# One over the softmax sums by the vector engine's reciprocal, in the attention of a hybrid encoder trunk

## The chip, the cores and the metric

The kernel runs on one core of a Trainium2 chip. The metric is the device time of one execution in microseconds (us). The core's engines each work through a queue of their own in order: TensorE (PE in the rows, PEld for its weight loads), the vector engine (DVE), the scalar engine (ACT), GpSimd (POOL), and the sync engine (SP), which issues the transfers.

## The reference

The program is a trunk of two layers over 1024 tokens of width 1024, in float32. Layer 0 mixes tokens by grouped-query attention, layer 1 by a gated linear attention; a squared-ReLU MLP follows each. The change lies in the attention alone:

```python
def block(qblk):
    s = jnp.einsum('bqhgd,bkhd->bhgqk', qblk, k, preferred_element_type=jnp.float32) * scale
    p = jax.nn.softmax(s, axis=-1).astype(v.dtype)
    return jnp.einsum('bhgqk,bkhd->bqhgd', p, v)
```

There are 16 query heads of width 64 and 4 key/value heads. The softmax of a row of scores is exp(s - max) divided by its sum; the division is what the change is about.

## The kernel before, in words

**Tiling.** The attention handles one head and one half of the queries (512 of 1024) at a time: 16 heads by 2 halves are 32 units, here called halves. A half has eight steps, one for each chunk of 128 keys. In a step `scores` lets TensorE write the scores of 128 keys by 512 queries into a PSUM bank `ps_a` (two matmuls, L389 and L390). ACT takes the exponential twice, once rounded into `ph` (L396) and once in full into `p` (L397), and `pl = p - ph` is made by DVE for even chunks and by POOL for odd ones (L400). Three steps later `values` multiplies `ph` and `pl` with the values (three matmuls, L109 to L111) and adds the result up in a bank `ps_c`, of which there are two.

**The end of a half.** The value matrix has 64 columns of ones beside its 64 value columns. So after the eighth chunk the bank holds the outputs on 64 partitions (`orow`) and the sum of the exponentials on the other 64 (`srow`), each 512 wide. The end of `values` divides one by the other (L423 to L427), rounds the quotient into `dst_h` (L429, named `oh` in the rows), moves it to other partitions for half of the heads (L432) and keeps the remainder in `dst_l` (L434, `ol`).

**The maxima ahead.** The row maximum that the softmax subtracts is found by a sweep of its own, 22 steps ahead (`LEAD`): `max_step` is one matmul (L276) into a bank `ps_b` (two of them), for every third into `ps_a` (four, shared with the scores), and a DVE reduction of 128x512 (L277). There are sixteen for a head, one for each step, so eight for a half; they stop when the last head has its maxima. `max_end` (L281 to L286) turns a head's maxima round by a small transposition (L283).

**What sets the order.** The code issues steps in the order of the loops, and a scheduler at build time then sorts each engine's queue. The order on every engine is fixed before the run. Four tiles each of `ph` and `pl` and three of `p` are in use in turn.

Of the kernel before, what the change touches and what calls it, by code (L numbers as in the profile page):

```python
# [25 lines left out]
AF = mybir.ActivationFunctionType  # L26
ALU = mybir.AluOpType
# [22 lines left out]
def trunk_kernel(tc, xT, wqk, wv, wo, win0, wout0, gqk, gv, gvz, gr, gate, gwo, win1, wout1, cols, rope, cmat, yT):  # L50
    nc = tc.nc
# [4 lines left out]
    with ExitStack() as top:  # L56
# [35 lines left out]
        def bank(tag):  # L92
            return psum.tile([P, HN], F32, tag=tag, name="ps_" + tag, bufs=PS_BUFS[tag])
# [14 lines left out]
        def mm3(ps, wh, wl, xh, xl, start, stop):  # L108
            nc.tensor.matmul(ps, wh, xh, start=start, stop=False)  # L109
            nc.tensor.matmul(ps, wh, xl, start=False, stop=False)  # L110
            nc.tensor.matmul(ps, wl, xh, start=False, stop=stop)  # L111
# [80 lines left out]
        with ExitStack() as at:  # L192
# [210 lines left out]
            def values():  # L403
                h, half, c, phh, pll = queue.pop(0)
                g = h // 4
                if c == 0:
                    out_bank[0] = bank("c")
                po = out_bank[0]
                two = slice(g % 2, g % 2 + 2)
                mm3(po, va[:, c, g // 2, two].rearrange("p a d -> p (a d)"), vb[:, c, g // 2, two].rearrange("p a d -> p (a d)"),  # L410
                    phh, pll, c == 0, c == NCH - 1)
                if c < NCH - 1:
                    return
                if h % 2 == 0:
                    oh[h // 2][half] = big.tile([P, HN], F32R, tag="hi", name="oh")
                    ol[h // 2][half] = big.tile([P, HN], F32R, tag="lo", name="ol")
                dst_h, dst_l = oh[h // 2][half], ol[h // 2][half]
                r0 = env.tmp.tile([P, HN], F32, tag="rs_r", name="r0")
                tt = env.tmp.tile([P, HN], F32, tag="rs_t", name="tt")

                top_, bot = slice(0, 64), slice(64, P)
                orow, srow = (bot, top_) if g % 2 else (top_, bot)
                nc.scalar.activation(out=r0[srow], in_=po[srow], func=AF.Ln)  # L423
                nc.scalar.activation(out=r0[srow], in_=r0[srow], func=AF.Exp, scale=-1.0)
                nc.vector.tensor_tensor(out=tt[srow], in0=po[srow], in1=r0[srow], op=ALU.mult)
                nc.vector.scalar_tensor_tensor(out=tt[orow], in0=tt[srow], scalar=-2.0, in1=r0[srow], op0=ALU.add, op1=ALU.mult)
                nc.vector.scalar_tensor_tensor(out=r0[orow], in0=po[orow], scalar=-1.0, in1=tt[orow], op0=ALU.mult, op1=ALU.mult)  # L427
                rows = bot if h % 2 else top_
                nc.scalar.copy(out=dst_h[rows], in_=r0[orow])  # L429
                src = r0  # L430
                if rows != orow:
                    nc.scalar.copy(out=tt[rows], in_=r0[orow])  # L432
                    src = tt
                nc.vector.tensor_tensor(out=dst_l[rows], in0=src[rows], in1=dst_h[rows].bitcast(F32), op=ALU.subtract)  # L434
# [3 lines left out]
            for step in range(256):  # L438
                h = step // 16
                scores(h, step // 8 % 2, step % 8)  # L440
                while unit < min(256, step + LEAD):
                    n, i = unit // 16, unit % 16
                    if i == 0:
                        if n % 4 == 0:
                            load_k(n // 4)
                        load_q(n)
                    max_step(n, i)
                    if i == 15:
                        max_end(n)
                    unit += 1  # L450
                if len(queue) > LAG:
                    values()
                if step == 200:
                    ahead = [load_w(wo[m]) for m in range(3)]
            begun = [proj("b", ahead[m], (oh, ol), 0) for m in range(2)]
            while queue:
                values()
# [817 lines left out]
```

## Time and profile before

| | |
|---|---|
| median of 3 runs | 2357.78 us (2353.15 to 2358.01) |
| the profiled execution's own time | 2352.89 us |
| span of its profile | 2350.8 us |
| TensorE's mean granted clock | 0.994 of full speed |
| busy over the span | TensorE 98%, DVE 76%, ACT 57%, POOL 14% |
| first and last line L425 (one for each half) | 195.65 and 559.4 us |

The busy share is a mean over stages with different limits. TensorE's matmuls are pipelined and their ends are modelled, so a matmul that starts every 0.23 us shows a duration of 0.4 us: starts, not durations, tell its pace. The span is 2.1 us shorter than the execution's time, for what lies before the first and after the last instruction.

### The profile page before, as it was taken

How to read it: one execution, taken by the hardware profiler on the slowest of the kernel's cores; microseconds unless marked ns; L12 is line 12 of the kernel's file. 1: busy time of each engine (PE TensorE's matmuls, PEld its weight loads, DVE VectorE, ACT ScalarE, POOL GpSimd, SP SyncE). 2: the span in 40 equal slices, each digit the busy share in tenths (PEclk: the TensorE clock that was granted, in tenths of full speed). 3: DMA queues.
4: the chain of work that ended last, by engine and by line, in shares of the span. 5: the costliest groups of instructions: out<-in, count | busy, mean ns of one | idle time of the engine just before them, and what ended most of it. 6: DMA issues, size and time to landing. Idle time of an engine off the chain costs nothing. (4 is left out here: it accounts for less than half of the span.)

```text
span 2350.8 us, 29858 instructions
## 1 busy us (share of the span) xinstructions
PE 2292.8 (98%) x10710; PEld 1898.6 (81%) x10710; DVE 1777.5 (76%) x2502; ACT 1341.4 (57%) x2386; POOL 333.2 (14%) x267
## 2 busy tenths in 40 slices
PE   8889999999999999999999999999999999999996
PEld 6677777777878888888888888898878888888885
DVE  8999999995786556888776767667696655897785
ACT  7458999994465555433344865655455555543343
POOL 2444444443000000000012000000100000000003
PEclk9999999999999999999999999999999999999998
DMA  4442112104445456954422121125625545965422
GB/s 173 135 146 64 42 41 52 30 14 165 132 160 180 152 175 228 320 166 160 153 99 81 47 74 54 55 72 187 220 91 194 177 152 182 331 204 177 154 89 72
DMA packets 157796, 317.50 MB, mean 135 GB/s; under 512 B 15048, under 2 KB 17872, under 8 KB 157520
## 3 DMA queue, kind: packets, MB, share of 16 engines
q1 hardware_dynamic: 157648, 315.60, 40.2%
q8 instruction: 84, 1.38, 0.2%
q14 instruction: 64, 0.52, 0.1%
HBM read 223.20 MB, written 92.27 MB: 134 GB/s over the span
## 5 line engine op out<-in xcount | busy, mean ns | idle before, releaser
L97 DVE TENSOR_TENSOR wl<-raw,wh 128x1024 fp32r<-128x1024 f32 x293 | 361.0, 1232 | 198.4 <-ACT wh L96 197.0
L96 ACT CAST wh<-raw 128x1024 fp32r<-128x1024 f32 x293 | 307.4, 1049 | 327.7 <-PE ps_a L466 130.6
L96 ACT CAST hh<-hst 128x512 fp32r<-128x512 f32 x224 | 134.9, 618 | 246.1 <-PE ps_a L467 112.4
L147 POOL TENSOR_TENSOR sq<-sq 128x512 f32<-128x512 f32 x35 | 54.6, 1560 | 1373.7 <-ACT sq L145 772.6
L400 POOL TENSOR_TENSOR pl<-p,ph 128x512 fp32r<-128x512 f32 x128 | 178.9, 1397 | 190.4 <-ACT p L397 136.4
L465 PE MATMUL ps_a<-xh,wh 128*128 128x512 f32 x512 | 199.6, 391 | 2.5 <-ACT xh L96 2.5
L467 PE MATMUL ps_a<-xh,wl 128*128 128x512 f32 x512 | 199.8, 391 | 1.8 <-DVE wl L97 1.8
L97 DVE TENSOR_TENSOR hl<-hst,hh 128x512 fp32r<-128x512 f32 x224 | 153.1, 703 | 62.9 <-ACT hh L96 62.1
L466 PE MATMUL ps_a<-xl,wh 128*128 128x512 f32 x512 | 200.5, 392 | 0.0
L465 PE MATMUL ps_a<-hh,wh 128*128 128x512 f32 x512 | 199.3, 389 | 1.1 <-ACT h L505 1.1
L466 PE MATMUL ps_a<-hl,wh 128*128 128x512 f32 x512 | 199.3, 389 | 0.6 <-DVE hl L97 0.6
L467 PE MATMUL ps_a<-hh,wl 128*128 128x512 f32 x512 | 199.2, 389 | 0.0
L396 ACT ACTIVATE ph<-ps_a 128x512 fp32r<-128x512 f32 x248 | 149.0, 601 | 22.2 <-PE ps_a L390 19.7
L397 ACT ACTIVATE p<-ps_a 128x512 f32<-128x512 f32 x256 | 153.1, 600 | 1.0 <-POOL pl L400 0.2
L465 PE MATMUL ps_b<-xh,wh 128*128 128x512 f32 x384 | 149.5, 389 | 0.2 <-DVE s L560 0.2
L467 PE MATMUL ps_b<-xh,wl 128*128 128x512 f32 x384 | 149.4, 389 | 0.0
L466 PE MATMUL ps_b<-xl,wh 128*128 128x512 f32 x384 | 149.4, 389 | 0.0
L277 DVE TENSOR_REDUCE mx<-ps_b 128x1 f32<-128x512 f32 x181 | 121.9, 682 | 7.6 <-PE ps_b L276 5.5
L505 ACT ACTIVATE s<-s 128x512 f32<-128x512 f32 x96 | 60.6, 631 | 105.9 <-DVE s L560 105.9
L465 PEld LDWEIGHTS ps_a<-xh,wh 128*128 128x128 f32 x512 | 96.4, 189 | 23.2 <-ACT xh L96 3.3
L467 PEld LDWEIGHTS ps_a<-xh,wl 128*128 128x128 f32 x512 | 96.5, 188 | 23.1 <-DVE wl L97 2.7
L465 PEld LDWEIGHTS ps_a<-hh,wh 128*128 128x128 f32 x512 | 96.1, 188 | 21.8 <-ACT h L505 1.7
(280 smaller groups left out, 6038.0 us busy)
## 6 DMA issues: line engine op xcount, KB each, us to landing
raw<-in_win_dram SPq DMA_DIRECT2D x80, 512.0 KB, 3.8
raw<-in_wout_dram SPq DMA_DIRECT2D x80, 512.0 KB, 3.9
hst<-hid_dramFalse SPq DMA_DIRECT2D x56, 512.0 KB, 3.8
hst<-hid_dramTrue SPq DMA_DIRECT2D x56, 512.0 KB, 3.5
q<-q_dram SPq DMA_DIRECT2D x96, 128.0 KB, 2.9
hid_dramFalse<-s SPq DMA_DIRECT2D x48, 256.0 KB, 2.1
hid_dramFalse<-t SPq DMA_DIRECT2D x48, 256.0 KB, 3.1
hid_dramTrue<-s SPq DMA_DIRECT2D x48, 256.0 KB, 2.0
```

The lines of the kernel that those rows point to most:

```text
L96: nc.scalar.copy(out=hi, in_=src)
L97: (leng or nc.vector).tensor_tensor(out=lo, in0=src, in1=hi.bitcast(F32), op=ALU.subtract)
L147: self.eng.tensor_tensor(out=sq, in0=self.acc, in1=sq, op=ALU.add)
L277: nc.vector.tensor_reduce(out=mx[h][:, half * 8 + c : half * 8 + c + 1], in_=ps, axis=AX.X, op=ALU.max, negate=True)
L396: nc.scalar.activation(out=phh, in_=ps, func=AF.Exp)
L397: nc.scalar.activation(out=p, in_=ps, func=AF.Exp)
L400: (nc.vector if c % 2 == 0 else nc.gpsimd).tensor_tensor(out=pll, in0=p, in1=phh.bitcast(F32), op=ALU.subtract)
L465: nc.tensor.matmul(ps, wh, xh, start=start and i == 0, stop=False, skip_group_check=not start)
L466: nc.tensor.matmul(ps, wh, xl, start=False, stop=False, skip_group_check=not start)
L467: nc.tensor.matmul(ps, wl, xh, start=False, stop=i == len(parts) - 1, skip_group_check=not start)
L505: nc.scalar.activation(out=t, in_=src, func=AF.Relu)
```

## The change

The logarithm and the exponential on ACT (L423, L424) go, and so do the three DVE instructions of the two Newton steps (L425 to L427). In their place DVE takes the reciprocal of the sums straight from the PSUM bank, from partitions `srow` into `tt` on partitions `orow`, and then multiplies the bank's outputs with it.

```diff
                 orow, srow = (bot, top_) if g % 2 else (top_, bot)
-                nc.scalar.activation(out=r0[srow], in_=po[srow], func=AF.Ln)
-                nc.scalar.activation(out=r0[srow], in_=r0[srow], func=AF.Exp, scale=-1.0)
-                nc.vector.tensor_tensor(out=tt[srow], in0=po[srow], in1=r0[srow], op=ALU.mult)
-                nc.vector.scalar_tensor_tensor(out=tt[orow], in0=tt[srow], scalar=-2.0, in1=r0[srow], op0=ALU.add, op1=ALU.mult)
-                nc.vector.scalar_tensor_tensor(out=r0[orow], in0=po[orow], scalar=-1.0, in1=tt[orow], op0=ALU.mult, op1=ALU.mult)
+                nc.vector.reciprocal(tt[orow], po[srow])
+                nc.vector.tensor_tensor(out=r0[orow], in0=po[orow], in1=tt[orow], op=ALU.mult)
                 rows = bot if h % 2 else top_
                 nc.scalar.copy(out=dst_h[rows], in_=r0[orow])
```

The two new lines are L423 and L424 of the changed kernel; the lines behind them stand three lower than before (the cast L429 is L426 there, the remainder L434 is L431). The queues change only within the attention; what comes ahead of it and behind it is the same, instruction for instruction, on every engine. Inside it, here is the queue of DVE at the end of the third half before the change, from one `pl` to the remainder:

```order
L400 TENSOR_TENSOR pl<-p,ph 128x512
L277 TENSOR_REDUCE mx<-ps_b 128x1
L425 TENSOR_TENSOR tt<-ps_c,r_2161 64x512
L277 TENSOR_REDUCE mx<-ps_b 128x1
L426 SCALAR_TENSOR_TENSOR tt<-tt,r_2161 64x512
L400 TENSOR_TENSOR pl<-p,ph 128x512
L427 SCALAR_TENSOR_TENSOR r_2161<-ps_c,tt 64x512
L277 TENSOR_REDUCE mx<-ps_a 128x1
L277 TENSOR_REDUCE mx<-ps_b 128x1
L434 TENSOR_TENSOR ol<-tt,oh 64x512
```

And the queue of DVE at the same place in the changed kernel:

```order
L400 TENSOR_TENSOR pl<-p,ph 128x512
L277 TENSOR_REDUCE mx<-ps_b 128x1
L423 RECIPROCAL tt<-ps_c 64x512
L281 TENSOR_TENSOR mx<-mx 128x8
L400 TENSOR_TENSOR pl<-p,ph 128x512
L424 TENSOR_TENSOR r_2155<-ps_c,tt 64x512
L277 TENSOR_REDUCE mx<-ps_b 128x1 x2
L431 TENSOR_TENSOR ol<-tt,oh 64x512
```

The three instructions that were spread between reductions and a `pl` are now two, with the reciprocal directly ahead of `max_end` and of a `pl`; what stands behind it, reductions and `pl` alike, is as many as before.

The second place is ACT's queue at the end of the same half, before:

```order
L423 ACTIVATE r_2161<-ps_c 64x512
L396 ACTIVATE ph<-ps_a 128x512
L285 CAST row<-ps_b 8x128
L424 ACTIVATE r_2161<-r_2161 64x512
L397 ACTIVATE p<-ps_a 128x512
```

and in the changed kernel, up to the cast of the quotient:

```order
L396 ACTIVATE ph<-ps_a 128x512
L285 CAST row<-ps_b 8x128
L397 ACTIVATE p<-ps_a 128x512
L426 CAST oh<-r_2155 64x512
L429 COPY tt<-r_2155 64x512
```

ACT no longer stands between TensorE's last matmul of a half and DVE; it meets the half again only at the cast of the finished quotient.

## Rows read from the trace of the kernel before

**Rows 1.** The page: busy us, share of the span, instructions of each engine.

```profile
PE 2292.8 (98%) x10710; PEld 1898.6 (81%) x10710; DVE 1777.5 (76%) x2502; ACT 1341.4 (57%) x2386; POOL 333.2 (14%) x267
```

**Rows 2.** Windows: from the 1st to the 29th end of a half, and the rest.

```profile
core 0: us, PE busy (x) PEld busy (x) DVE busy (x) ACT busy (x) POOL busy (x), PEclk, DMA share, GB/s
195.65:519.79 324.14, 321.15 (x1360) 252.86 (x1360) 303.32 (x462) 294.03 (x564) 156.52 (x112) 1.00 0.15 38
519.79:570.00 50.21, 48.75 (x209) 38.66 (x208) 32.70 (x40) 27.79 (x50) 17.64 (x13) 1.00 0.23 74
```

**Rows 3.** Timeline of DVE over one half: start us, duration us, instruction.

```profile
265.33 0.69 DVE L425 TENSOR_TENSOR tt<-ps_c,r 64x512 f32<-64x512 f32 x1 [0.40 <-ACT r L424]
266.06 0.69 DVE L277 TENSOR_REDUCE mx<-ps_b 128x1 f32<-128x512 f32 x1
266.66 1.17 DVE L426 SCALAR_TENSOR_TENSOR tt<-tt,r 64x512 f32<-64x512 f32 x1
267.87 0.69 DVE L400 TENSOR_TENSOR pl<-p,ph 128x512 fp32r<-128x512 f32 x1
268.48 0.68 DVE L427 SCALAR_TENSOR_TENSOR r<-ps_c,tt 64x512 f32<-64x512 f32 x1
269.08 0.67 DVE L277 TENSOR_REDUCE mx<-ps_a 128x1 f32<-128x512 f32 x1
269.67 0.67 DVE L277 TENSOR_REDUCE mx<-ps_b 128x1 f32<-128x512 f32 x1
...
276.82 0.69 DVE L425 TENSOR_TENSOR tt<-ps_c,r 64x512 f32<-64x512 f32 x1 [0.41 <-ACT r L424]
```

**Rows 4.** Timeline of PE within that half, from one L110 to the next but one.

```profile
265.67 0.40 PE L110 MATMUL ps_c<-pl,va 128*128 128x512 f32 x1
265.90 0.40 PE L111 MATMUL ps_c<-ph,vb 128*128 128x512 f32 x1
...
268.46 0.40 PE L110 MATMUL ps_c<-pl,va 128*128 128x512 f32 x1
```

**Rows 5.** Groups of DVE and ACT, 195.65 to 519.79: busy us, mean ns, idle ahead.

```profile
L277 DVE TENSOR_REDUCE mx<-ps_b 128x1 f32<-128x512 f32 x154 | 104.0, 682 | 6.1 <-PE ps_b L276 4.0
L400 DVE TENSOR_TENSOR pl<-p,ph 128x512 fp32r<-128x512 f32 x112 | 82.3, 735 | 3.1 <-ACT p L397 1.7
L426 DVE SCALAR_TENSOR_TENSOR tt<-tt,r 64x512 f32<-64x512 f32 x28 | 29.7, 1060 | 0.4
L425 DVE TENSOR_TENSOR tt<-ps_c,r 64x512 f32<-64x512 f32 x28 | 19.3, 688 | 8.9 <-ACT r L424 8.7
L427 DVE SCALAR_TENSOR_TENSOR r<-ps_c,tt 64x512 f32<-64x512 f32 x28 | 19.2, 684 | 0.4
L434 DVE TENSOR_TENSOR ol<-tt,oh 64x512 fp32r<-64x512 f32 x14 | 9.6, 687 | 0.6 <-ACT tt L432 0.2
L424 ACT ACTIVATE r<-r 64x512 f32<-64x512 f32 x28 | 17.6, 630 | 0.6
L423 ACT ACTIVATE r<-ps_c 64x512 f32<-64x512 f32 x28 | 16.6, 592 | 0.4
```

**Rows 6.** Waits, 195.65 to 519.79: us in total, times, longest us.

```profile
PEld ps_b L283 <- DVE mx L281: 8.4, 14, 0.9
PE ps_b L283 <- DVE mx L281: 2.9, 7, 0.5
```

**Rows 7.** The group with DVE's longest time per element, over the whole span.

```profile
L974 DVE TENSOR_TENSOR_SCAN lg<-ones_f,lg 128x128 f32<-128x128 f32 x64 | 21.8, 405 | 0.3
```

**Rows 8.** Windows of 4 us ahead of the attention, columns as in rows 2.

```profile
100.00:104.00 4.00, 0.87 (x3) 0.19 (x1) 4.00 (x4) 1.69 (x3) 3.05 (x2) 1.00 0.63 184
104.00:108.00 4.00, 3.71 (x11) 2.96 (x12) 3.88 (x7) 1.20 (x3) 0.00 (x0) 0.66 0.00 0
108.00:112.00 4.00, 4.00 (x18) 3.21 (x17) 4.00 (x6) 2.67 (x6) 2.83 (x2) 0.91 0.93 321
```

## The prediction

> **What bounds the kernel now.** The page comes first: TensorE is busy for 98% of the span, DVE for 76%, ACT for 57% [rows 1]. That is a mean over the whole program, while the change touches one stage only, so the next view is the stage alone: the window from the 1st to the 29th end of a half [rows 2]. It holds 28 halves in 324.14 us, 11.58 us each, and it is the stretch in which every half also has its eight reductions for the maxima. After the 29th end the reductions are over and DVE is busy for only 32.7 of 50.2 us.
>
> In that window three engines are close to full at once: TensorE 321 of 324 us, DVE 303, ACT 294 [rows 2]. The busy share can't say which of them sets the pace, so I read the starts. On TensorE a matmul starts every (268.46 - 265.67)/12 = 0.2325 us when nothing holds it [rows 4]. The 1360 matmuls of the window, 14 of them small transpositions, then take some 316.5 us: 11.30 us for a half. That is TensorE's floor, and the window is 7.6 us above it.
>
> DVE's timeline shows instructions back to back, a new one every 0.60 us in a run of reductions, though each lasts 0.67 to 0.69 [rows 3]. Its waits on named engines in the window are 8.7 us for ACT's exponential L424, 4.0 for TensorE, 1.7 for `p` and 0.2 for L432 [rows 5], 14.6 us in all. So DVE needs (324.14 - 14.6)/28 = 11.05 us of each half's 11.58. The reader should see two queues in lockstep: TensorE with a floor of 11.30 and DVE with 11.05. A saving on DVE can buy at most TensorE's 7.6 us; an extra load on DVE is covered for only a quarter of a microsecond per half and must be paid for beyond that.
>
> **The change part by part.**
>
> *ACT.* L423 and L424 go: 0.592 + 0.630 = 1.22 us of each half [rows 5]. ACT had about a tenth of the window idle already, so this buys only what waited for it: DVE's 8.7 us ahead of L425, 0.31 us a half, inside DVE's time and not beside it.
>
> *DVE, removed.* L425, L426 and L427: 0.688 + 1.060 + 0.684 = 2.43 us a half [rows 5].
>
> *DVE, added, known.* The product of the PSUM outputs with the reciprocal has the shape and the operands of L427, so 0.684 us. Without the reciprocal DVE is then at 11.05 - 2.43 + 0.68 = 9.30 us a half. It stays hidden behind TensorE's 11.30 as long as the reciprocal takes less than 2.00 us. That is the point from which everything decides.
>
> *DVE, added, unknown.* No row of this trace is a reciprocal. From below: any other DVE instruction on 64x512 takes 0.69 us [rows 5]. The longest time per element on DVE is the scan, 405 ns for 128 elements; four such are 1.62 us [rows 7]. From above I count what the program now spends on one over the sums and its product. The four instructions that yield the inverse take 0.592 + 0.630 + 0.688 + 1.060 = 2.97 us [rows 5]. Counted as arithmetic, the five lines make seven operations on each element (logarithm, exponential, product, addition, product, sign, product); at one pass of 0.60 us for each [rows 3] that is 4.2 us. The ends are far apart. A quotient to full precision is a chain of dependent steps, and each DVE row here does one or two steps in a pass; that puts it nearer to the counted chain than to one addition. I take 3.7 us, between 2.97 and 4.2, and keep 0.69 and 4.2 as bounds.
>
> [...]
>
> *The sum in the window.* 9.30 + 3.7 = 13.0 us of DVE work in each half. This is above TensorE's 11.30, so DVE sets the pace: (13.0 - 11.58) x 28 = +40 us. Nothing is double-counted here: the 14.6 us of waits vanish, since a DVE that is behind finds its inputs ready.
>
> *Who is behind the reciprocal.* In DVE's queue of the changed kernel stand a `max_end`, a `pl` and reductions behind it. While it runs, TensorE can put maxima into the two `ps_b` banks and perhaps one `ps_a`, about three steps' worth; then the next L276 has no bank, or an L110 has no `pl` for its even chunk, and since TensorE's queue is in order the next scores wait too, and ACT with them. After it DVE works off the backlog at 0.60 us each, and TensorE goes on at DVE's pace. So the stall appears on TensorE as waits on DVE, which now come only from the transposition of the maxima, 2.9 us in the window [rows 6]. It can't be caught up, as every later half starts with TensorE already as far ahead as the banks allow.
>
> *After the 29th end.* Three reciprocals remain. DVE has 17 us idle in those 50 [rows 2], so their sum fits; but a `pl` stuck behind 3.7 us is as late as the lead of three steps (three times five matmuls at 0.2325, 3.5 us). Price between 0 and 2 us each, I take 1: +3 us.
>
> *Moves.* The order differs within the attention only, no transfer is added or removed, and POOL's queue is the same; I price that at 0. Its cover is that queues around it stay behind the same matmuls; if it fails, the waits on L276 and L110 grow, which the range holds.
>
> In all +43 us on the profiled execution's 2352.9: 2396 us. That execution lies 4.9 us under the median of the three runs, which would give 2401. I forecast **2398 us**, 1.7% slower.
>
> **The rivals.**
>
> *The reciprocal is a single pass (0.69 to 1.6 us); it ends on the other side.* For it: ACT's rows do even a logarithm in one pass of 0.592 us [rows 5]. Against it: DVE's rows do no more than two plain operations in a pass. DVE falls to 10.0 to 10.9 us a half, TensorE sets the pace at 11.30, and at most 28 x (11.58 - 11.30) = 7.8 us come back: 2345 to 2352 us. It decides at 2.00 us a reciprocal. [...] Chance 0.12.
>
> *About break-even (1.8 to 2.3 us).* Neither end of my counts lies there. DVE and TensorE tie, and the time stays at 2350 to 2362. Chance 0.05.
>
> [...] Chance 0.24.
>
> *The stall also costs TensorE its clock.* The granted clock is 1.00 throughout the window now. [...] Against it: the stall is 1.4 us a half and comes in pieces, bank by bank. Chance 0.05.
>
> **How the numbers follow.** My forecast (reciprocal between 2.9 and 4.2 us, 2372 to 2412) has 0.50, eight passes 0.24, the clock 0.05, break-even 0.05, the single pass 0.12, and some 0.04 is left for an order that hurts by itself, 2360 to 2375. A range from 2372 to 2428 leaves out the single pass, break-even, and some of the clock and the order: a little under 0.2. About 0.2%, 5 us, is what a measurement of this kernel can tell from no change. Of the single pass three quarters are faster by that much; with a little for the unforeseen, faster 0.10, same 0.09, slower 0.81.
>
> **What would show it.** The reciprocal's own row decides first: 3 to 4.3 us on 64x512, 32 times. Then the window from the 1st to the 29th end grows to 360 us or so, with DVE busy for nearly all of it and TensorE's share falling to about 88%; TensorE's waits on L277 and L400 grow from 3 us to tens; ACT's idle time grows by what it lost plus the stall; the stretches before 190 us and after the attention keep their lengths to within 2 us. I am wrong if the reciprocal's row is below 2.0 us, and wrong in mechanism if it is above 3 and the window still keeps 324 us, for then DVE was not as full as its starts say.

## The result, and the profile after

The changed kernel takes 2393.36 us (median of 4 runs, 2391.07 to 2395.85), the kernel before 2356.68 (4 runs): ratio 1.016, 95% interval 1.0145 to 1.0176. It is 37 us slower; the forecast was 2398. The profiled execution is the slowest of its four, 2395.85 us.

The page of the changed kernel, busy us of each engine, answers to [rows 1]:

```profile
PE 2312.8 (97%) x10710; PEld 1892.6 (79%) x10710; DVE 1835.8 (77%) x2470; ACT 1309.6 (55%) x2322; POOL 330.0 (14%) x267
```

The shares hardly move; who reads only these sees nothing. The windows of the stage, from the 1st to the 29th end of a half and behind it, answer to [rows 2]:

```profile
core 0: us, PE busy (x) PEld busy (x) DVE busy (x) ACT busy (x) POOL busy (x), PEclk, DMA share, GB/s
196.09:557.77 361.68, 337.86 (x1364) 246.12 (x1365) 354.87 (x434) 266.72 (x508) 153.88 (x113) 1.00 0.12 35
557.77:607.00 49.23, 46.99 (x198) 35.75 (x197) 38.46 (x36) 24.16 (x43) 18.07 (x13) 1.00 0.20 68
```

The 28 halves take 361.68 us where they took 324.14, 12.92 us each for 11.58: this is +37.5 us, nearly all of the loss. DVE is now busy for 98% of the window, ACT has 95 us idle in it for 30, and the granted clock stayed at 1.00. The first end starts 0.4 us later than before. The groups of DVE in that window, with mean ns and idle time, answer to [rows 5]:

```profile
L277 DVE TENSOR_REDUCE mx<-ps_b 128x1 f32<-128x512 f32 x154 | 102.3, 679 | 0.6
L423 DVE RECIPROCAL tt<-ps_c 64x512 f32<-64x512 f32 x29 | 97.3, 3355 | 0.9
L400 DVE TENSOR_TENSOR pl<-p,ph 128x512 fp32r<-128x512 f32 x112 | 88.2, 787 | 3.0 <-ACT p L397 1.1
L424 DVE TENSOR_TENSOR r<-ps_c,tt 64x512 f32<-64x512 f32 x28 | 19.2, 685 | 0.7
L431 DVE TENSOR_TENSOR ol<-r,oh 64x512 fp32r<-64x512 f32 x14 | 11.8, 845 | 0.4 <-ACT oh L426 0.2
```

The reciprocal takes 3.355 us, five times a product of the same shape. DVE hardly waits any more: the reductions stood idle for 6.1 us in [rows 5], now for 0.6. And two lines that the change doesn't touch have become slower: `pl` from 735 to 787 ns, the remainder of half of the heads from 685 to 845. TensorE's waits in the same window (us in total, times, longest) answer to [rows 6]:

```profile
PE ps_c L110 <- DVE pl L400: 10.6, 24, 0.7
PE ps_a L389 <- DVE mx L277: 7.7, 12, 0.9
PE ps_b L283 <- DVE mx L281: 2.5, 9, 0.5
```

What stood behind the reciprocal in DVE's queue is what TensorE now waits for: `pl` of the even chunks and the banks that the reductions hold. With two shorter waits the named ones add up to 22 us.

One half on DVE, start us and duration us, answers to [rows 3]:

```profile
259.81 3.36 DVE L423 RECIPROCAL tt<-ps_c 64x512 f32<-64x512 f32 x1
263.19 0.69 DVE L277 TENSOR_REDUCE mx<-ps_a 128x1 f32<-128x512 f32 x1
263.80 0.67 DVE L424 TENSOR_TENSOR r<-ps_c,tt 64x512 f32<-64x512 f32 x1
264.40 0.68 DVE L400 TENSOR_TENSOR pl<-p,ph 128x512 fp32r<-128x512 f32 x1
...
265.60 0.67 DVE L431 TENSOR_TENSOR ol<-r,oh 64x512 fp32r<-64x512 f32 x1
...
266.80 1.35 DVE L400 TENSOR_TENSOR pl<-p,ph 128x512 fp32r<-128x512 f32 x1
268.08 0.67 DVE L277 TENSOR_REDUCE mx<-ps_a 128x1 f32<-128x512 f32 x1
```

There is no gap in it. POOL's timeline over the same stretch:

```profile
261.73 1.29 POOL L400 TENSOR_TENSOR pl<-p,ph 128x512 fp32r<-128x512 f32 x1 [1.15 <-ACT p L397]
265.70 1.91 POOL L400 TENSOR_TENSOR pl<-p,ph 128x512 fp32r<-128x512 f32 x1 [2.68 <-ACT p L397]
```

DVE's `pl` at 264.40 has POOL idle beside it and takes 0.68 us. POOL's `pl` at 265.70 begins while DVE's remainder L431 runs and takes 1.91 for its usual 1.29; DVE's `pl` at 266.80 begins while POOL's still runs and takes 1.35. The ends show what happens: POOL's ends at 267.61, 1.3 us after the remainder, and DVE's at 268.15, 0.54 us after POOL's. So here the one that starts second is held until the first has ended. Of the 37 `pl` on DVE in the changed kernel that start while POOL's has more than 0.15 us to go, 36 end 0.54 to 0.55 us after it, though POOL's had between 0.24 and 1.13 us to go when they started. All of DVE's `pl` sorted by whether POOL's ran beside it for more than 0.3 us: 0.98 us on average when it did (51 of them), 0.69 when it did not (77). The reductions, which read a single operand from PSUM, take 0.68 either way, and the product L424, with one operand in PSUM and one in SBUF, 0.69.

The kernel before has the same collision at another line. Its L426 reads two SBUF operands (shortest, median and longest ns), and in [rows 3] it starts at 266.66, beside this `pl` of POOL:

```profile
L426 DVE SCALAR_TENSOR_TENSOR tt<-tt,r x32: 685/1160/1648, 197.0 to 560.1; 64x512 f32<-64x512 f32 x32
266.00 1.29 POOL L400 TENSOR_TENSOR pl<-p,ph 128x512 fp32r<-128x512 f32 x1 [2.73 <-ACT p L397]
```

It ends at 267.83, 0.54 us after POOL's. Of its 32 instances 29 start inside a `pl` of POOL and end 0.54 to 0.56 us after it.

### The profile page after: what moved, and what is told of

The parts are those of the page before. It is cut to its first block, busy times and chain, and to the rows that moved or that the text cites. A ratio compares the mean times of both kernels' runs of the same rounds, so it can differ in the third digit from the quotient of the medians.

```text
span 2393.8 us, 29883 instructions
## 1 busy us (share of the span) xinstructions
PE 2312.8 (97%) x10710; PEld 1892.6 (79%) x10710; DVE 1835.8 (77%) x2470; ACT 1309.6 (55%) x2322; POOL 330.0 (14%) x267
## 5 line engine op out<-in xcount | busy, mean ns | idle before, releaser
L400 POOL TENSOR_TENSOR pl<-p,ph 128x512 fp32r<-128x512 f32 x128 | 176.7, 1380 | 235.0 <-ACT p L397 128.8
L110 PE MATMUL ps_c<-pl,va 128*128 128x512 f32 x256 | 105.8, 413 | 12.7 <-DVE pl L400 11.3
```

The source lines that it names most:

```text
L400: (nc.vector if c % 2 == 0 else nc.gpsimd).tensor_tensor(out=pll, in0=p, in1=phh.bitcast(F32), op=ALU.subtract)
```

## The experiments

Theory A is that of the prediction: DVE's sum of work sets the pace of a half as soon as it is above TensorE's floor of 11.30 us. Rival B is that the reciprocal costs by what it blocks while it runs, however much room DVE has. A third question is the slower `pl`. Ratios are to the kernel before, on the same chip; differences to the changed kernel in us are between chips, which differ by some 2 us for the kernel before.

**e1, half the width**: the reciprocal of 256 columns, used twice.

```diff
-nc.vector.reciprocal(tt[orow], po[srow])
+nc.vector.reciprocal(tt[orow, :256], po[srow, :256])
...
+    in1=tt[orow, None, :256].to_broadcast([64, 2, 256]), op=ALU.mult)
```

> Leaves out the reciprocal of the second 256 columns: the first 256 are used twice. Theory A (DVE's load sets the pace): a reciprocal of 256 columns takes about half of 3.36 us, 1.7, below the break-even of 2.0; DVE needs 12.87 - 1.66 = 11.2 us a half, under TensorE's floor of 11.30 with its few waits, and the time falls to 2350 to 2358 us. Rival B (the reciprocal costs by what it blocks, in proportion to its length, and not by DVE's sum): half of the 37 us stays, about 2375 us.

Measured 2378.64 us, ratio 1.0103 (1.0088 to 1.0118): A's number missed, B's nearly met. The groups of DVE in its 28 halves:

```profile
L400 DVE TENSOR_TENSOR pl<-p,ph 128x512 fp32r<-128x512 f32 x112 | 96.1, 858 | 2.6 <-ACT p L397 1.1
L423 DVE RECIPROCAL tt<-ps_c 64x256 f32<-64x256 f32 x28 | 49.2, 1756 | 0.9
L432 DVE TENSOR_TENSOR ol<-r,oh 64x512 fp32r<-64x512 f32 x14 | 15.8, 1132 | 0.3
L432 DVE TENSOR_TENSOR ol<-tt,oh 64x512 fp32r<-64x512 f32 x14 | 14.6, 1040 | 0.3
L281 DVE TENSOR_TENSOR mx<-mx 128x8 f32<-128x8 f32 x14 | 7.5, 538 | 0.0
```

The reciprocal shrank as expected, but the remainder now takes over 1.0 us, `pl` 0.86 and the tiny L281 0.54 for 0.17. DVE was still nearly full: 12.09 us of work in halves of 12.41. B came near its number, but DVE's sum had not fallen as I assumed. That pointed to POOL.

**e2, spread**: four pieces of 128 columns, one after each of the next four chunks.

```diff
+def piece(i):
+    qs = slice(i * P, i * P + P)
+    nc.vector.reciprocal(tt[orow, qs], po[srow, qs])
...
+ends.extend([partial(piece, i) for i in range(4)] + [rest])
```

> The reciprocal in four pieces of 128 columns, one behind each of the next four chunks, the product behind the fifth. Theory A: DVE's sum stays or grows by the pieces' fixed part (3 x 0.1 us a half at most): 2390 to 2402 us. Rival B: no piece holds DVE for longer than 0.9 us, less than one step, so TensorE's stall goes and the time falls to 2370 us or below.

Measured 2424.19 us, ratio 1.0296 (1.0280 to 1.0311), 31 us slower than in one piece. B is refuted: no reciprocal holds DVE for longer than 0.96 us and the loss nearly doubles. A has the direction, but its number was 22 us too low. The groups:

```profile
L431 DVE RECIPROCAL tt<-ps_c 64x128 f32<-64x128 f32 x112 | 106.8, 955 | 3.3
L400 DVE TENSOR_TENSOR pl<-p,ph 128x512 fp32r<-128x512 f32 x112 | 97.9, 874 | 1.4
```

Four pieces are 3.82 us for 3.36, a reduction and what follows it start 0.68 us apart for 0.65, and `pl` (874 ns for 787) and the remainder (864 for 765 over both rows) are slower again. By half that is 0.46 + 0.2 + 0.35 + 0.1 us, for a half that grew from 12.92 to 14.04. DVE needs 14.02 us a half.

**e3, no POOL `pl`**: `ph` stands in for odd chunks; otherwise the changed kernel.

```diff
+if c % 2 == 0:
+    nc.vector.tensor_tensor(out=pll, in0=p, in1=phh.bitcast(F32), op=ALU.subtract)
+else:
+    pll = phh
```

> Leaves out POOL's subtraction for odd chunks: ph stands in for pl in TensorE's matmul, so TensorE's work is the same and POOL is idle in the attention. If DVE's L400 and L431 are slower after the change (787 and 845 ns where 735 and 687 were) because POOL works at the same time: both fall to about 0.69 us, DVE's sum falls by 0.25 to 0.4 us a half, and the time by 7 to 11 us, to 2382 to 2386. If POOL has no part in it: 2390 to 2396 us.

Measured 2378.95 us, ratio 1.0103 (1.0086 to 1.0120): 14 us faster than the changed kernel, more than expected: `pl` by 105 ns, four times a half, and the remainder by 80 are the 0.50 us a half by which DVE's sum fell. All of DVE's `pl` in it, with the shortest, median and longest ns:

```profile
L401 DVE TENSOR_TENSOR pl<-p,ph x128: 669/682/694, 182.2 to 574.2; 128x512 fp32r<-128x512 f32 x128
```

Not one is slow, where the changed kernel's reach 1.67 us: the slow ones come from POOL's work. A `pl` takes 0.68 us here with POOL idle, and in the changed kernel 0.98 on average with POOL beside it; a reduction from PSUM takes 0.68 either way.

**e5, both**: half the width and no POOL `pl`, the edits of e1 and e3.

> Leaves out both the second half of the reciprocal and POOL's subtraction for odd chunks (ph stands in for pl). With the reciprocal at its measured 1.74 us for 256 columns, DVE's other instructions at their lengths without POOL beside them sum to 5.2 (reductions) + 2.5 (pl) + 0.7 (product) + 0.7 (remainder) + 0.05, 10.9 us a half in all. If POOL's work beside DVE's is what kept the half-width kernel at 12.41 us a half: TensorE's floor of 11.3 to 11.5 decides, and the time falls to 2345 to 2355 us. If the length of the blocked stretch or the new order kept it there: 2370 us or above.

Measured 2349.17 us, ratio 0.9976 (0.9966 to 0.9985), as A had it. DVE's sum is 10.81 us, and a half takes 11.40. The two groups that had grown in e1:

```profile
L401 DVE TENSOR_TENSOR pl<-p,ph 128x512 fp32r<-128x512 f32 x112 | 75.9, 678 | 3.7 <-ACT p L397 2.1
L435 DVE TENSOR_TENSOR ol<-r,oh 64x512 fp32r<-64x512 f32 x14 | 9.5, 682 | 0.3
```

The reciprocal of e5 is as long as that of e1, 1.755 us, and in e1 no instruction of TensorE has a named wait for POOL's `pl`. So the collisions of DVE with POOL are what kept e1 slow.

**e6, all `pl` on POOL** in the changed kernel.

```diff
-(nc.vector if c % 2 == 0 else nc.gpsimd).tensor_tensor(out=pll, ...
+nc.gpsimd.tensor_tensor(out=pll, in0=p, in1=phh.bitcast(F32), op=ALU.subtract)
```

> The changed kernel with every pl on POOL: eight a half at 1.29 us are 10.3 us, under TensorE's floor. DVE keeps reductions 5.2, reciprocal 3.34, product 0.66, remainder 0.7 to 1.1: 10.0 to 10.4 us a half. If DVE's sum sets the pace (theory A): the loss goes and the time is 2345 to 2358 us. If the reciprocal costs by blocking (rival B), reductions still stand behind it for 3.4 us and 2375 us or more remains. If POOL becomes the bound through being late with pl: above 2360 us, with TensorE waiting for POOL's L400.

Measured 2362.23 us, ratio 1.0036 (1.0024 to 1.0049): the full reciprocal of 3.355 us is there, in one block, and 29 of the 37 us are gone: 8 are left over the kernel before on the same chip. A's number was missed by 4 us, B's by 13. The third branch, POOL late with `pl`, has the number but not its sign: TensorE has no named wait for POOL's L400, though POOL is busy for 87% of the window. The rest has a row among the groups of DVE:

```profile
L281 DVE TENSOR_TENSOR mx<-mx 128x8 f32<-128x8 f32 x14 | 13.1, 936 | 0.3
```

and TensorE has one wait in the window (us in total, times, longest):

```profile
PE ps_b L283 <- DVE mx L281: 8.5, 8, 2.3
```

L281 combines eight columns of two SBUF operands, 0.17 us when undisturbed; here it takes 0.94, and TensorE's transposition waits for it. The 16 instances take between 0.24 and 2.57 us. That POOL's `pl` holds them, as it holds DVE's `pl`, is my reading of this spread; no row shows the two side by side. The window is 11.2 us longer than that of e9 below, and 8.5 of them are this wait.

**e7, all `pl` on POOL** in the kernel before, the same edit.

> The kernel before with every pl on POOL: DVE falls from 11.05 to about 9 us a half, so TensorE's floor of 11.30 us decides and up to 7 us can be won: 2345 to 2352 us against 2354. If the floor is not TensorE's, or POOL is late with pl, 2355 us or above.

Measured 2358.31 us, ratio 1.0018 (1.0009 to 1.0028): a miss. DVE's sum fell to 9.16 us, but the halves stayed at 11.58. TensorE's one named wait in the window:

```profile
PE ps_b L283 <- DVE mx L281: 4.7, 7, 1.0
```

L281 takes 0.63 us on average here, for 0.17 in e9, where POOL makes only half of the `pl`; that POOL holds it is again my reading. The window of 324.26 us is 5.6 longer than that of e9, so this wait is most of what keeps it there; none of TensorE's matmuls has a named wait for POOL's `pl`. The other 4 us over the kernel before lie outside the window and are not settled.

**e4 and e8, ACT's part.** e4 keeps logarithm and exponential beside the reciprocal.

```diff
+nc.scalar.activation(out=r0[srow], in_=po[srow], func=AF.Ln)
+nc.scalar.activation(out=r0[srow], in_=r0[srow], func=AF.Exp, scale=-1.0)
```

> The logarithm and exponential are kept on ACT beside the reciprocal, their result unused. Theory A: ACT has over a quarter of the window idle and nothing waits for these two, so the time stays at 2390 to 2397 us: what the change took off ACT bought nothing. Rival C (ACT's load shares the path, through the exponentials that TensorE and POOL wait for): up to 1.22 us a half, +10 to +34 us, 2403 to 2427.

In e8 ACT copies the sums to SBUF, and the reciprocal reads them there.

```diff
-nc.vector.reciprocal(tt[orow], po[srow])
+nc.scalar.copy(out=r0[srow], in_=po[srow])
+nc.vector.reciprocal(tt[orow], r0[srow])
```

> ACT first copies the sums to SBUF, and the reciprocal reads them there. ACT has over a quarter of the window idle. If the reciprocal's 3.355 us are its own arithmetic (6.25 ns a column in the three widths): the same 3.3 us, or some 0.06 less or more for the other memory, and 2390 to 2405 us. If reading PSUM slows it: clearly below 3 us, and at 1.7 us (two columns at a time) some 2378 us, like the half width.

e4 took 2399.62 us, ratio 1.0197 (1.0180 to 1.0213): 6 us over the changed kernel, a little above A's bracket and far below C's full price. Its DVE sum is 12.93 us, near the changed kernel's 12.87, but DVE waits 7.0 us in the window for 1.4, all of it for ACT's `p` and its copies of the quotient. So the relief of ACT was worth some 6 us, or 9 by the ratios, through DVE's waits. e8 took 2400.86, ratio 1.0200 (1.0184 to 1.0215). Its reciprocal:

```profile
L424 DVE RECIPROCAL tt<-r x32: 3346/3347/3349, 195.2 to 604.6; 64x512 f32<-64x512 f32 x32
```

3.347 us from SBUF, 3.355 from PSUM: where it reads from hardly matters for its length. The 0.06 us allowed for the other memory was my estimate, and no run shows it.

**e10, twice**: a second, identical reciprocal.

```diff
+nc.vector.reciprocal(tt[orow], po[srow])
```

> A second, identical reciprocal behind the first, work done twice. Theory A: 3.35 us more of DVE in each half, 94 us in the window and at most 3.4 for each of the 3 or 4 ends behind it: 2487 to 2500 us. Rival B (TensorE's stall depends on the longest single block): clearly less, 2450 us or below.

One run, 2502.79 us, 109 us above the changed kernel, where 32 more reciprocals of 3.355 us are 107; A's bracket of 2487 to 2500 was missed by 3. Its window and the row of `pl`:

```profile
202.50:669.56 467.06, 386.42 (x1373) 284.30 (x1374) 455.98 (x463) 269.82 (x507) 149.84 (x112) 0.88 0.09 25
L400 DVE TENSOR_TENSOR pl<-p,ph 128x512 fp32r<-128x512 f32 x113 | 98.1, 868 | 0.7
```

A half takes 16.68 us and DVE's sum is 16.47. The window grew by 105 us where 94 were added: `pl`, at 868 ns for 787, is 9 us of the rest, and DVE waits 6.0 us for 1.4, while the remainder is 2 us shorter. The granted clock over the window is 0.88, where it was 1.00 in the changed kernel: a half is now 5.4 us above TensorE's 11.30, and in part of the window the clock is about half of full speed (0.52 from 316 to 320 us, behind 4 us in which TensorE was busy for 2.15). DVE's waits are all for ACT's copies of the quotient and none for TensorE, so the slower TensorE was covered here.

**e9, without the Newton steps**, from the kernel before: logarithm and exponential on ACT, written straight to the outputs' partitions, and one product. The inverse is then only as sharp as ACT makes it.

```diff
+nc.scalar.activation(out=tt[orow], in_=r0[srow], func=AF.Exp, scale=-1.0)
+nc.vector.tensor_tensor(out=r0[orow], in0=po[orow], in1=tt[orow], op=ALU.mult)
```

> The logarithm and the exponential alone, multiplied in, without the two Newton steps that sharpen them. DVE loses L425 and L426, 0.71 + 1.11 = 1.8 us a half, and is at 9.2 us; ACT is as before. If TensorE's floor of 11.30 us was worked out rightly: the window goes from 11.58 to 11.3 to 11.4 a half, and the time to 2346 to 2351 us, 3 to 8 under the kernel before. If ACT or another queue is the real limit beside DVE: no change, 2353 to 2356 us.

Measured 2346.02 us, ratio 0.9964 (0.9950 to 0.9977). It is faster than both kernels, at the price of the sharpening that it leaves out. Its window from the 1st to the 29th product:

```profile
195.75:514.45 318.70, 318.70 (x1360) 253.37 (x1360) 264.97 (x406) 293.20 (x564) 144.74 (x112) 1.00 0.14 38
```

TensorE has no idle time and no named wait left; a half takes 11.38 us, close to the floor of 11.30 that was read from the starts.

**e11, the remainder on POOL**, in the kernel before.

```diff
-nc.vector.tensor_tensor(out=dst_l[rows], in0=src[rows], ...
+nc.gpsimd.tensor_tensor(out=dst_l[rows], in0=src[rows], ...
```

> The kernel before with the remainder L434 on POOL in place of DVE. DVE loses 0.66 us a half, POOL gains some 0.7 to 1.3. If room on DVE alone is worth something: 2348 to 2353 us. If POOL's extra work stretches the DVE instructions that run beside it (L400, L426) by as much as was saved: 2353 to 2357 us.

Measured 2355.89 us, ratio 1.0003 (0.9995 to 1.0012): nothing won. The row of `pl` on DVE shows why:

```profile
L400 DVE TENSOR_TENSOR pl<-p,ph 128x512 fp32r<-128x512 f32 x113 | 101.0, 894 | 3.8 <-ACT p L397 1.6
```

735 ns before, 894 now: 0.64 us for the four of a half, which is what moving the remainder (0.66) had saved. So no room was made on DVE, and what room alone is worth in the kernel before this run cannot say.

All runs together. DVE's sum is the window less its waits on named engines, over 28 halves; for the experiments the window goes from the 1st to the 29th product:

| kernel | DVE's sum, us a half | a half takes, us |
|---|---|---|
| e7 all `pl` on POOL, from before | 9.16 | 11.58 |
| e9 without Newton | 9.64 | 11.38 |
| e6 all `pl` on POOL, from after | 10.44 | 11.78 |
| e5 half width, no POOL `pl` | 10.81 | 11.40 |
| e11 remainder on POOL | 11.03 | 11.56 |
| before | 11.05 | 11.58 |
| e1 half width | 12.09 | 12.41 |
| e3 no POOL `pl` | 12.37 | 12.58 |
| after | 12.87 | 12.92 |
| e4 ACT's two kept | 12.93 | 13.19 |
| e8 from SBUF | 13.07 | 13.20 |
| e2 spread | 14.02 | 14.04 |
| e10 twice | 16.47 | 16.68 |

The difference of the two columns is DVE's waits by the way the sum is made, so the table alone shows no cause: it says that DVE hardly waits wherever its sum is above 11.3 us (0.35 us a half at most). The cause is shown by what was taken off DVE or added to it: e3, e5, e6 and e10. Below 11.3 us the half stays at 11.4 to 11.8 whatever DVE has left.

## Why the prediction was right

**What bounds the stage: shown for the changed kernel, argued for the one before.** That DVE's sum sets the changed kernel's pace, and that TensorE's floor is near 11.30, is shown by e3, e5, e6, e10 and by e9. That the kernel before stood in lockstep, with DVE's 11.05 beside the floor, is not: e7 took 1.9 us a half off DVE and the half stayed at 11.58. TensorE's waits for L281 are 2.9 us of the 5.4 by which that window exceeds e9's; the rest is open.

**The reciprocal's length: 3.355 us for the 3.7 taken**, inside the bounds of 0.69 and 4.2 but by a count that has no claim to be the mechanism: that it came so near is luck. Its three widths (0.955, 1.756 and 3.355 us for 128, 256 and 512 columns) give 6.25 ns a column and 0.16 us fixed. The rivals of a single pass, of break-even and of eight passes fall with this row. No run shows the eight passes, to which the forecast gives 0.24 and which its range of 2372 to 2428 us takes in: what the runs show in their place is 3.355 us, 5.6 times the 0.60 us between the starts of two reductions in [rows 3].

**The break-even of 2.00 us did not hold.** e1's reciprocal takes 1.756 us and the kernel is still 24 us slower than before; only with POOL idle as well (e5) did it fall under the floor. The step behind it is the next one.

**The rest of DVE's work: the step that was mis-sized.** "Without the reciprocal DVE is then at 11.05 - 2.43 + 0.68 = 9.30 us a half" took every other line at its old length. It measured 12.87 - 3.34 = 9.53 us, with 3.34 from start to start. The sign stood in [rows 5]: "any other DVE instruction on 64x512 takes 0.69 us" passes over L426 with its 1060 ns. L426 was the line that met POOL's `pl`; with it gone, 37 of DVE's `pl` begin inside one of POOL's, where 25 did. The errors cancel in part, which is luck too: (3.34 - 3.7) x 28 = -10 us, (9.53 - 9.30) x 28 = +6, and waits of 1.4 us that I had set to nothing. Of the window's forecast +40 came +37.5.

**The waits** of DVE fell from 14.6 to 1.4 us, and TensorE's stalls stand where they were expected, on L110 and on banks held by reductions; e2 shows that the length of the block was not what cost. ACT's part was more than DVE's 8.7 us: e4 puts 6 to 9 us on it in the changed kernel. One sign was missed: TensorE's share fell to 93% and not to 88%, as a busy share counts 0.4 us for a matmul that starts 0.2325 after the last.

**After the 29th end** I had +3 us. From there to the first sum of the next stage out of `ps_a` (564.1 us before, 603.2 after) it is 45.4 for 44.3 us: +1.1.

**Elsewhere.** The two profiled spans differ by 43.0 us, the window, the start and the tail by 39.1. The other 3.9 us lie behind the attention, where the code is the same and I had allowed 2. Most of them are the clock's. Two stretches of the changed kernel, and the same places in the kernel before, with columns as in [rows 2]:

```profile
722.00:725.40 3.40, 3.40 (x8) 2.72 (x9) 3.40 (x6) 0.41 (x1) 0.00 (x0) 0.52 0.42 154
1292.00:1295.40 3.40, 3.40 (x10) 2.66 (x9) 1.86 (x4) 1.54 (x3) 1.20 (x1) 0.52 0.58 152
683.20:686.60 3.40, 3.40 (x15) 2.82 (x16) 3.40 (x6) 0.43 (x1) 0.00 (x0) 1.00 0.55 154
1250.80:1254.20 3.40, 3.40 (x17) 2.81 (x16) 2.93 (x6) 1.88 (x3) 1.18 (x1) 1.00 0.57 158
```

At 0.52 and 1.00 TensorE starts 8 and 15, 10 and 17 matmuls in 3.4 us: some 3 us lost in the two. In the 4 us ahead TensorE was busy for 1.86 and 2.28 us in the changed kernel, for 1.88 and 2.29 in the kernel before, so why the clock fell in the one alone stays open, and these 3 us cannot be put down to the change.

**The clock** in the window stayed at 1.00 with a stall of 1.3 us a half. The rival of a slower clock, with 0.05, did not come here: no run shows a loss of clock from the stall of one reciprocal a half; in e10 the clock did fall, to 0.88, but behind a DVE that was full.

## What to carry to other kernels

Where two engines run in lockstep, work out both sums for one turn of the loop from starts and waits, and price a replaced operation against the room that is left. Moving work between DVE and POOL is not a sum of rows: here 36 of 37 `pl` of DVE in the changed kernel, and all 29 L426 in the kernel before, that began while POOL's subtraction had more than 0.15 us to go ended 0.54 to 0.56 us after it, and in e11 `pl` grew from 735 to 894 ns, which gave the whole saving back. A row whose mean lies well above the others of its shape, as L426 with 1060 ns, is the sign to look for. Before replacing several cheap instructions by one, measure that one in its own width: DVE's reciprocal took 3.355 us on 64x512, five products of 0.685.

## What was not expected of the hardware

DVE's instructions with two SBUF operands and POOL's subtraction did not slow each other down but took turns: a `pl` of DVE that began inside one of POOL ended 0.55 us after it (36 of 37 in the changed kernel), for a length of 0.68 alone. So the loss is not in proportion to an instruction's size: one on 8 columns took 0.94 us on average, and 2.57 at most, where POOL was busy for 87% of the window (e6), and 0.17 before. And cutting a blocking DVE instruction into pieces made the kernel 31 us slower. A piece of a quarter's width took 0.955 us, where a quarter of 3.355 is 0.84; that is 13 of the 31 us, and the rest is in the instructions around the pieces.
